# A two-layer encoder trunk on one core: one folded map at the start, value shifts issued by SyncE, the mask inside the running product, and dense matmuls pinned beside the last attention

## The chip, the core and the metric

The kernel runs on one core of a Trainium2 chip. A core has five engines with a queue each: TensorE (matmuls, PE in the profile; PEld is its weight load), VectorE (DVE), ScalarE (ACT), GpSimd (POOL) and SyncE (SP), which here does nothing but issue DMAs. ScalarE's queue can issue DMAs too. Each queue is worked off in order, so an instruction that waits holds back those behind it. Data lie in SBUF (128 partitions) and in DRAM; matmuls write to PSUM banks. The metric is the time of one execution in microseconds (us).

## The reference

All is float32: 2048 positions, 1024 channels, 16 heads of 64.

```
layer A: h = rms_norm(x); u, z = h @ w_in
         pooled = (trailing means of u over 2, 4, 8, 16 positions, by channel group) - u
         x += ((pooled per group @ w_group) * scale * silu(z)) @ w_out;  x += (p0 @ ple0) * sigmoid(x @ gate0)
k, v  = rms_norm(x) @ w_kv;  k = rms_norm per head
layer B: q, z = rms_norm(x) @ w_in;  q = rms_norm per head
         A[t,s] = beta[t,s] * prod_{s<j<t} (1 - beta[t,j]),  beta = sigmoid(q.k / 8),  only s < t
         o = A @ v;  x += (o * silu(z)) @ w_out;  x += (p1 @ ple1) * sigmoid(x @ gate1)
```

## The kernel before, in words

**Matmuls.** Each operand is split into a high part and the rest (`hi`, `lo`), and a product is three matmuls per 128 channels: hi x hi (L221), hi x lo (L223), lo x hi (L226). A dense product of 128 outputs by 512 positions is thus 24 matmuls of 512 columns in one PSUM bank `psd`. The first two products of a stage go through `product2` (L240, L242, L245); q, k and v through `kvq` (L467).

**Chunks.** The 2048 positions are four chunks of 512. For a chunk, `first_part` runs layer A: `mixer` (z and pooled u per group, 16 products), `out_steps` (8), `gate_steps` (8 and 8 small ones), then z of layer B (`gate_z`, 8) and q, k, v of heads 0 to 7; `second_part` runs q, k, v of heads 8 to 15. Before u is needed, `fold` multiplies the input map of a group with its group map (48 matmuls of 256 columns, L271), and the result `wf` goes to DRAM and comes back as weights.

**Attention** runs in slots (chunk c, head h, key chunk kc from c down to 0), each of four steps j, one per 128 queries. In a step `front` makes logits (L690, L691, bank `psl`), ScalarE their sigmoid of the negative (L693, `pp`), in the slot on the diagonal GpSimd sets the masked keys to 1 (L695), and VectorE runs the product along the keys from last to first (L697). `turn` transposes the result by four matmuls (L708, `psa`), ScalarE and VectorE split it into `at` (L711, L712), and `gather` multiplies with values (L720, L721, `pso`). Since A is a difference of two neighbours of the running product, the values enter as differences of neighbouring rows: `valued` (L480 to L490) makes a row-shifted copy `vs` of v by DMAs, on ScalarE's queue, stores the last row of each 128 (`ve`), and `load_ends` (L678) reads these back as `en`.

**What sets the order.** The code is one stream of dense matmuls (`stream`, a generator that yields after each) into which attention steps are cut: in each step `fill` draws a share of the stream that `rate` gives, 66 products per chunk spread over the chunk's steps. `until` runs the stream on to the mark after which a head's q, k, v exist. What is written so is then put in order by a scheduler, which may bring any instruction forward whose inputs it takes to be ready. After the last chunk's attention, `post(3)` (output projection and gate of layer B, 18 products' worth) is left. `post(0)` to `post(2)` are filler of the last attention.

**Weights** come as units, nine in flight (`UNITS`), in the order of a list `plan`: at first use raw from DRAM into an `io` buffer, cast and split by ScalarE with VectorE or GpSimd (L129 to L136), and stored once; later uses load the stored pair (L143). `io` also holds x, residuals and others.

Of the kernel before, what the change touches and what calls it, by code (L numbers as in the profile page):

```python
# [36 lines left out]
def trunk_kernel(ctx, tc, x, p, a_norm, wu_t, wz_a, w_group, a_scale, a_w_out, kv_norm, w_kv,  # L37
# [11 lines left out]
    zeros = cp.tile([P, 1], F32, name="zeros")  # L49
    V.memset(zeros, 0.0)  # L50
# [33 lines left out]
    io = flat("io", 5)  # L84
# [11 lines left out]
    state = {"solo": True, "turn": 0, "lo": 0}  # L96
# [27 lines left out]
    wq = {"out": 0, "back": 0, "cap": 2, "by": nc.scalar}  # L124
# [69 lines left out]
    for s in range(NSUB):  # L194
        if s == 0:
            plan_group(3)
            plan_group(2)
        for g in (3, 2, 1, 0):
            plan_block("za", wz_a, g, g_a, True)
            plan_block("wf", None, g)  # L200
            if s == 0 and g > 1:
                plan_group(g - 2)
# [47 lines left out]
    def fold(g):  # L250
        parts = {}
        raws = {}
        for h in range(2):
            for c in range(2):
                raws[c, h] = raw = io("uraw")
                nc.sync.dma_start(out=raw, in_=wu_t[2 * g + c, :, h * W5 : (h + 1) * W5])
        (wg, _), = take(1)
        for h in range(2):
            for c in range(2):
                raw = raws[c, h]  # L260
                hi, lo = ppt("uh", F32R), ppt("ul", F32R)
                A.copy(out=hi, in_=raw)
                V.tensor_tensor(out=lo, in0=raw, in1=f(hi), op=ALU.subtract)
                parts[c, h] = (hi, lo)
        for kts in PAIRS:
# [28 lines left out]
    def token_norm(total, nm):  # L294
        ps = turned()
        for j in range(4):
            T.matmul(ps[:, 0, j : j + 1], total[:, j * P : (j + 1) * P], ones, start=True, stop=True)
        ss = pool.tile([P, 4], F32, tag="ss" + nm, name="ss")
# [24 lines left out]
    def prep(s):  # L323
        ck = chunk[s]
        ck["x"] = []
        for o in range(KT):
# [8 lines left out]
            gather_squares(ck, "acc1", o, xin)  # L335
            yield
        r = token_norm(ck["acc1"], "x")
# [39 lines left out]
    def mixer(s):  # L377
        ck = chunk[s]
        ck["m"] = {}
        for g in (3, 2, 1, 0):  # L380
            us, zs = take(4), []
            for k in range(2):
                ps = dense()
                yield from product(ps, us, ck["x"], k * P, k)
                zs.append(silu(ps, ck["rb1"]))
            us = take(4)
# [4 lines left out]
            if s == 0 and g > 1:  # L391
                yield from fold(g - 2)
# [65 lines left out]
    def kvq(s, kind, b):  # L458
        ck = chunk[s]
        us = take(KT)  # L460
        for j in range(4):
            tk = slice(j * P, (j + 1) * P)
            ps = dense()
            for kt in range(KT):
                u = us[kt][0]
                for xh, wh in ((0, 0), (1, 0), (0, 1)):
# [4 lines left out]
                    yield  # L471
                if lag and (j, kt) in ((1, 2), (1, 5), (2, 1), (2, 4)):
# [5 lines left out]
    def valued(s, kind, b, j, ps, rj):  # L478
# [3 lines left out]
        for lo, hi in ((0, 112), (112, P - 1)):  # L482
            nc.scalar.dma_start(out=vs[lo + 1 : hi + 1], in_=vr[lo:hi])
        if j:
            nc.scalar.dma_start(out=vs[0:1], in_=chunk[s]["vr"][P - 1 : P])
        elif s:
            nc.scalar.dma_start(out=vs[0:1], in_=ve[s - 1][b][3:4])
        else:
            V.memset(vs[0:1], 0.0)
        nc.scalar.dma_start(out=ve[s][b][j : j + 1], in_=vr[P - 1 : P])  # L490
# [65 lines left out]
    def gate_z(s):  # L556
# [8 lines left out]
        us = take(4)  # L565
        pss = [dense(), dense()]
        yield from product2(pss, us, ck["x2"])
        first = []
        for k in range(2):
            zr = row("zr")  # L570
            A.copy(out=zr, in_=pss[k])
            first.append(zr)
        ck["r2"] = token_norm(ck["acc2"], "y")
        for b in range(1, 4):
            us = take(4)
            for k in range(2):
                o = 2 * b + k
                ps = dense()
                for i, _ in enumerate(product(ps, us, ck["x2"], k * P, k)):
                    if o == 2 and i == 20:  # L580
# [11 lines left out]
    def first_part(s):  # L592
# [6 lines left out]
        yield from every(gate_z(s), 48, ck["side"])  # L599
# [3 lines left out]
        marks.add((s, 0))  # L603

# [70 lines left out]
    def load_ends(c, b):  # L675
        en = pool.tile([P, 4, 4], F32, tag="en", name="en")
        for j in range(4):
            nc.scalar.dma_start(out=en[:, :, j], in_=ve[c][b][j].rearrange("(m q) -> q m", q=P))  # L678
# [5 lines left out]
    def front(st, j):  # L684
# [9 lines left out]
        if st["diag"]:  # L694
            G.affine_select(out=pp[:, W5 - P :], in_=pp[:, W5 - P :], pattern=[[-1, P]], compare_op=ALU.is_gt,  # L695
# [206 lines left out]
```

## Time and profile before

| | |
|---|---|
| median of 3 runs | 2842.41 us (2839.97 to 2845.93) |
| the profiled execution | 2844.09 us, its span 2842.3 us |
| granted TensorE clock, mean | 0.983 |
| busy: TensorE, VectorE, ScalarE, GpSimd | 2729.0, 1863.5, 1267.3, 1012.1 us |
| matmuls | 13344 |
| DMA | 651.86 MB, mean 229 GB/s |

A row of the grouped view has line, engine, operation, out<-in, shapes and count, then busy time in us and mean ns of one, then the engine's idle time before them and what ended most of it. A row of the timeline has start and duration in us, engine ("q" behind it: its sequencer, which issues DMAs), line, operation, names, count, and in brackets the idle time before it with its releaser. A row of the view by stretches has, for each engine, busy us and number of instructions. A row on a line's operation has the shortest, median and longest duration in ns, and the first and last start.

### The profile page before, as it was taken

The numbers are of one execution on the slowest core, as the hardware profiler recorded it, in microseconds if no ns is written. First come the engines' busy times: TensorE is split into PE (matmuls) and PEld (weight loads), VectorE is DVE, ScalarE is ACT, GpSimd is POOL, SyncE is SP. The second block draws the span as 40 slices with busy tenths as digits, with TensorE's granted clock in tenths as the row PEclk, the third lists the DMA queues.
The fourth block names the chain that finished last, engine by engine and source line by source line (L and its number), as shares of the span: only waits on it lengthen the run. The fifth ranks groups of instructions, "written<-read, shape, count | busy, mean of one in ns | idle before, by whom it ended". The sixth has DMA issues, their size and how long they took to land. (4 is left out here: it accounts for less than half of the span.)

```text
span 2842.3 us, 39230 instructions
## 1 busy us (share of the span) xinstructions
PE 2729.0 (96%) x13344; PEld 2247.5 (79%) x13344; DVE 1863.5 (66%) x2369; ACT 1267.3 (45%) x2498; POOL 1012.1 (36%) x961
## 2 busy tenths in 40 slices
PE   7999979989999999999999999999999999998889
PEld 6888867877878888887888877787788888886567
DVE  6745445757344787655577887665667777678962
ACT  5335443444444345444444554444444344445541
POOL 2454433767543355543324452323212121111112
PEclk9999999999999999999999999999999999999999
DMA  7748799878887745678684548457697776763335
GB/s 294 269 148 302 295 337 351 305 246 294 296 289 278 238 143 176 219 228 273 229 271 152 155 155 261 157 200 241 212 288 230 218 256 210 235 204 111 108 117 184
DMA packets 302804, 651.86 MB, mean 229 GB/s; under 512 B 51462, under 2 KB 84230, under 8 KB 302604
## 3 DMA queue, kind: packets, MB, share of 16 engines
q1 hardware_dynamic: 278080, 639.23, 67.9%
q10 hardware_dynamic: 24524, 10.11, 1.5%
q8 instruction: 106, 1.74, 0.3%
q14 instruction: 94, 0.77, 0.1%
HBM read 479.82 MB, written 161.02 MB: 225 GB/s over the span
## 5 line engine op out<-in xcount | busy, mean ns | idle before, releaser
L697 DVE TENSOR_TENSOR_SCAN pp<-pp,zeros 128x512 f32<-128x512 f32 (+3 forms) x640 | 778.5, 1236 | 239.1 <-ACT pp L693 118.9
L467 PE MATMUL psd<-wpair,x 128*128 128x512 f32 x2304 | 589.5, 398 | 17.5 <-ACT wpair L135 8.1
L467 PEld LDWEIGHTS psd<-wpair,x 128*128 128x128 f32 x2304 | 428.4, 190 | 108.8 <-ACT wpair L135 9.2
L712 DVE TENSOR_TENSOR at<-psa,at 128x512 fp32r<-128x512 f32 (+3 forms) x640 | 373.9, 597 | 198.4 <-ACT at L711 196.9
L711 ACT CAST at<-psa 128x512 fp32r<-128x512 f32 (+3 forms) x640 | 330.2, 525 | 376.0 <-PE psa L708 344.2
L693 ACT ACTIVATE pp<-psl 128x512 f32<-128x512 f32 (+3 forms) x640 | 325.3, 534 | 288.6 <-PE psl L691 149.5
L708 PE MATMUL psa<-ident,pp 128*128 128x128 f32 x2176 | 354.5, 279 | 47.7 <-DVE at L712 42.4
L708 PEld LDWEIGHTS psa<-ident,pp 128*128 128x128 f32 x2176 | 273.7, 143 | 135.4 <-DVE at L712 50.1
L695 POOL TENSOR_SCALAR_AFFINE_SELECT pp<-pp 128x128 f32<-128x128 f32 x256 | 119.1, 469 | 544.3 <-ACT pp L693 517.1
L721 PE MATMUL pso<-at,vv 128*128 128x512 f32 (+3 forms) x640 | 271.8, 425 | 0.2 <-DVE at L712 0.2
L690 PE MATMUL psl<-kk,qa 128*128 128x512 f32 (+3 forms) x640 | 244.4, 384 | 4.5 <-ACT pp L693 4.0
L720 PE MATMUL pso<-at,vv 128*128 128x512 f32 (+3 forms) x640 | 240.2, 376 | 6.5 <-ACT at L711 3.9
L691 PE MATMUL psl<-kk,qb 128*128 128x512 f32 (+3 forms) x640 | 234.7, 369 | 0.0
L221 PE MATMUL psd<-x,wpair 128*128 128x512 f32 x576 | 228.7, 397 | 4.9 <-ACT sg L443 3.4
L223 PE MATMUL psd<-x,wpair 128*128 128x512 f32 x576 | 227.3, 395 | 0.0
L226 PE MATMUL psd<-x,wpair 128*128 128x512 f32 x576 | 227.1, 394 | 0.0
L221 PE MATMUL psd<-xp,wpair 128*128 128x512 f32 x512 | 201.0, 393 | 1.4 <-DVE ub L356 0.6
L223 PE MATMUL psd<-xp,wpair 128*128 128x512 f32 x512 | 200.6, 392 | 0.0
L226 PE MATMUL psd<-xp,wpair 128*128 128x512 f32 x512 | 200.2, 391 | 0.0
L131 POOL TENSOR_TENSOR wpair<-wraw,wpair 128x512 fp32r<-128x512 f32 x98 | 142.3, 1458 | 93.3 <-ACT wpair L129 92.9
L690 PEld LDWEIGHTS psl<-kk,qa 128*128 128x128 f32 x640 | 122.4, 191 | 32.0 <-ACT pp L693 12.7
L720 PEld LDWEIGHTS pso<-at,vv 128*128 128x128 f32 x640 | 123.5, 193 | 24.6 <-ACT at L711 9.4
(159 smaller groups left out, 4761.4 us busy)
## 6 DMA issues: line engine op xcount, KB each, us to landing
wpair<-once SPq DMA_DIRECT2D x384, 512.0 KB, 5.6
once<-wpair SPq DMA_DIRECT2D x80, 512.0 KB, 6.5
kk<-kd SPq DMA_DIRECT2D x320, 128.0 KB, 3.4
vv<-vd SPq DMA_DIRECT2D x160, 256.0 KB, 4.0
wpair<-wf SPq DMA_DIRECT2D x64, 512.0 KB, 5.4
once<-kp SPq DMA_DIRECT2D x36, 512.0 KB, 5.4
wraw<-in_a_w_out_dram SPq DMA_DIRECT2D x64, 256.0 KB, 3.8
wraw<-in_gate_a_dram SPq DMA_DIRECT2D x64, 256.0 KB, 4.2
```

Source lines behind the costliest of these rows:

```text
L221: T.matmul(ps, hi, acts[kt][:, 0], start=(i == 0), stop=False)
L223: T.matmul(ps, hi, acts[kt][:, 1], start=False, stop=False)
L226: T.matmul(ps, lo, acts[kt][:, 0], start=False, stop=(i == n))
L467: T.matmul(ps, ck["x2"][kt][:, xh, tk], u[:, wh, 0], start=(kt == 0 and xh == wh), stop=(kt == KT - 1 and wh == 1))
L690: T.matmul(ps[:, :w], qa[:, qs], kk[:, :w], start=True, stop=False)
L693: A.activation(out=pp[:, r0:], in_=ps[:, :w], func=AF.Sigmoid, scale=-1.0)
L697: V.tensor_tensor_scan(out=pp[:, r0:][:, ::-1], data0=pp[:, r0:][:, ::-1], data1=zeros.to_broadcast([P, w]), initial=1.0 if st["diag"] els ...
L708: T.transpose(pt[:, j * P : (j + 1) * P], pp[:, r0 + kt * P : r0 + (kt + 1) * P], ident)
L711: A.copy(out=at[:, 0, cs], in_=pt[:, cs])
L712: V.tensor_tensor(out=at[:, 1, cs], in0=pt[:, cs], in1=f(at[:, 0, cs]), op=ALU.subtract)
L720: T.matmul(po[:, cs], vv[:, kt, :], at[:, 0, cs], start=(st["diag"] and kt == 0), stop=False)
L721: T.matmul(po[:, cs], vv[:, kt, :], at[:, 1, cs], start=False, stop=(st["last"] and kt == 3))
```

## The change

Six things are edited.

1. **Start.** The input map of group 3 alone is folded before x is read in; those of groups 2, 1 and 0 are loaded one group ahead (`fold_load`) and folded at the start of their own group, not two groups ahead. The sums of squares of the first chunk's x are made by 32 one-column matmuls (L355 in the new file) instead of additions on GpSimd. The first weights are asked for with a cap of 1, not 2.
2. **Shifts.** The DMAs of `valued` and `load_ends` are issued by SyncE instead of ScalarE.
3. **Mask.** The select on GpSimd (256 of them) goes. The running product takes the larger of the product and a floor, where it added zero: the floor is 0, and 1 at masked keys. It is a constant tile of 512 columns, and `io` has 4 buffers instead of 5.
4. **Last z.** In the last chunk `gate_z` runs after q, k, v of heads 0 to 7 and behind the mark that lets attention start. The norm it used to make is made in `kvq`.
5. **Rate.** Accordingly 58 products are spread over the third chunk's attention, and 74 over the last.
6. **Pins.** Beside the last attention, each first matmul of a weight unit in `product` stays behind the matmul written before it on TensorE.

```diff
-    zeros = cp.tile([P, 1], F32, name="zeros")
-    V.memset(zeros, 0.0)
+    floor = cp.tile([P, W5], F32, name="floor")
+    V.memset(floor, 0.0)
+    G.affine_select(out=floor[:, W5 - P :], in_=floor[:, W5 - P :], pattern=[[-1, P]], compare_op=ALU.is_gt,
+                    fill=1.0, base=0, channel_multiplier=1)
-    io = flat("io", 5)
+    io = flat("io", 4)
-    wq = {"out": 0, "back": 0, "cap": 2, "by": nc.scalar}
+    wq = {"out": 0, "back": 0, "cap": 1, "by": nc.scalar}
...
+        if s + 1 == NSUB:
+            plan_kvq(0)
         for b in range(4):
             plan_block("zb", b_w_z, b, g_b, True)
-        plan_kvq(0)
+        if s + 1 < NSUB:
+            plan_kvq(0)
...
-                T.matmul(ps, hi, acts[kt][:, 0], start=(i == 0), stop=False)
+                ins = T.matmul(ps, hi, acts[kt][:, 0], start=(i == 0), stop=False)
+                if state["pin"] and e == 0:
+                    tc.keep_in_program_order(ins)
...
+                sq = tmp("sq")
+                A.activation(out=sq, in_=xin, func=AF.Square)
+                if o == 0:
+                    sums = turned()
+                for j in range(4):
+                    tc.keep_in_program_order(
+                        T.matmul(sums[:, 0, j : j + 1], sq[:, j * P : (j + 1) * P], ones,
+                                 start=(o + j == 0), stop=(o == KT - 1 and j == 3)))
...
         for g in (3, 2, 1, 0):
+            if s == 0 and g < 3:
+                yield from fold(g)
...
+            if s == 0 and g:
+                fold_load(g - 1)
...
-            if s == 0 and g > 1:
-                yield from fold(g - 2)
...
+                if j == 0 and kt == 5 and "r2" not in ck:
+                    ck["r2"] = token_norm(ck["acc2"], "y")
...
-            nc.scalar.dma_start(out=vs[lo + 1 : hi + 1], in_=vr[lo:hi])
+            nc.sync.dma_start(out=vs[lo + 1 : hi + 1], in_=vr[lo:hi])
...
-        yield from every(gate_z(s), 48, ck["side"])
+        if s + 1 < NSUB:
+            yield from every(gate_z(s), 48, ck["side"])
         for kind in "qkv":
             yield from every(kvq(s, kind, 0), 48, ck["side"])
         settle()
         marks.add((s, 0))
+        if s + 1 == NSUB:
+            yield from gate_z(s)
...
-            nc.scalar.dma_start(out=en[:, :, j], in_=ve[c][b][j].rearrange("(m q) -> q m", q=P))
+            nc.sync.dma_start(out=en[:, :, j], in_=ve[c][b][j].rearrange("(m q) -> q m", q=P))
...
-        if st["diag"]:
-            G.affine_select(out=pp[:, W5 - P :], in_=pp[:, W5 - P :], pattern=[[-1, P]], compare_op=ALU.is_gt,
-                            fill=1.0, base=0, channel_multiplier=1)
-        V.tensor_tensor_scan(out=pp[:, r0:][:, ::-1], data0=pp[:, r0:][:, ::-1],
-                             data1=zeros.to_broadcast([P, w]),
-                             initial=1.0 if st["diag"] else st["carry"][j], op0=ALU.mult, op1=ALU.add)
+        least = floor[:, r0:][:, ::-1] if st["diag"] else floor[:, 0:1].to_broadcast([P, w])
+        V.tensor_tensor_scan(out=pp[:, r0:][:, ::-1], data0=pp[:, r0:][:, ::-1], data1=least,
+                             initial=1.0 if st["diag"] else st["carry"][j], op0=ALU.mult, op1=ALU.max)
...
-        return (66 * 24.0) / (64 * (c + 1) - (5 if c < NSUB - 1 else 0))
+        parts = 66 + (0, 0, -8, 8)[c]
+        return (parts * 24.0) / (64 * (c + 1) - (5 if c < NSUB - 1 else 0))
...
+            state["pin"] = slots[i][0] == NSUB - 1
```

**Where the order moves: the last attention.** On TensorE, at the transposes of the twelfth head of the last chunk; before:

```order
L708 MATMUL psa_25766<-ident_60,pp_25652 128x128
L708 MATMUL psa_25766<-ident_60,pp_25677 128x128
L708 MATMUL psa_25766<-ident_60,pp_25704 128x128
L721 MATMUL pso_25385<-at_25723,vv_25473 128x512
L690 MATMUL psl_25893<-kk_25726,qa_25499 128x512
L691 MATMUL psl_25893<-kk_25726,qb_25500 128x512
L690 MATMUL psl_25918<-kk_25726,qa_25499 128x512
L691 MATMUL psl_25918<-kk_25726,qb_25500 128x512
```

and now, at the same head:

```order
L736 MATMUL psa_24960<-ident_60,pp_24915 128x128
L749 MATMUL pso_24592<-at_24907,vv_24689 128x512
L721 MATMUL psl_24992<-kk_24827,qa_24714 128x512
L722 MATMUL psl_24992<-kk_24827,qb_24715 128x512
L230 MATMUL psd_24953<-og_24272,wpair_24590 128x512
L223 MATMUL psd_24953<-og_24274,wpair_24615 128x512
L227 MATMUL psd_24953<-og_24274,wpair_24615 128x512
L230 MATMUL psd_24953<-og_24274,wpair_24615 128x512
L223 MATMUL psd_24953<-og_24276,wpair_24615 128x512
L748 MATMUL pso_24592<-at_24932,vv_24689 128x512
```

The dense products (`psd`), which had run out four heads earlier, now stand between the steps. Counted from one head's first transposes to the next head's, the last chunk's first 15 heads have 132, 120, 120, 136, 128, 120, 136, 132, 122, 66, 6, 0, 6, 0, 6 dense matmuls before, and 90, 73, 101, 115, 102, 118, 109, 115, 106, 122, 101, 111, 111, 67, 6 now; behind the 16th stands what is left of the end. In the chunk before, where a head has 12 steps, the two leanest stretches of 16 steps go from 63 and 88 to 48 and 99.

**ScalarE's queue at the start** (`uh` is the high part of the input map, `wraw` and `wpair` the group map, `xp` the first x). Before:

```order
L146 DMA wraw_322<-in_a_w_group_dram 128x512
L262 ACT_TABLE_LOAD
L262 CAST uh_331<-uraw_313 128x512
L320 DMA xin_359<-in_x_dram 128x512
L262 CAST uh_335<-uraw_315 128x512
L320 DMA xin_363<-in_x_dram 128x512
L146 DMA wraw_327<-in_a_w_group_dram 128x512
L262 CAST uh_339<-uraw_317 128x512
L129 CAST wpair_321<-wraw_322 128x512
L776 DMA gains_103<-in_a_scale_dram 128x8
```

and now:

```order
L331 DMA xin_359<-in_x_dram 128x512
L266 CAST uh_332<-uraw_320 128x512
L148 DMA wraw_341<-in_a_w_group_dram 128x512
L806 DMA gains_106<-in_a_scale_dram 128x8
L266 CAST uh_336<-uraw_322 128x512
L806 DMA gains_106<-in_b_norm_dram 128x8
L806 DMA gains_106<-in_kv_norm_dram 128x8
L806 DMA gs_108<-in_k_norm_dram 128x1
L806 DMA gs_108<-in_b_q_norm_dram 128x1
L131 CAST wpair_340<-wraw_341 128x512
L119 CAST xp_496<-xin_345 128x512
```

One group map is loaded instead of two, behind the third cast, and its own cast stands behind the loads of the five gains. On TensorE, 24 of the 32 sums stand between the map's matmuls and the first dense one, the last eight 13 dense matmuls further.

**SyncE's queue at the first value block** (`vr` is a block of 128 value rows). Before, these DMAs were ScalarE's, and SyncE went from `qa`, `qb` to `once` and `wraw`. Now:

```order
L690 DMA qa_3637<-qd0_0_229 64x512
L515 DMA ve0_0_301<-vr_3396 1x512
L508 DMA vs_3398<-vr_3396 112x512
L508 DMA vs_3398<-vr_3396 15x512
L508 DMA vs_3464<-vr_3462 112x512
L508 DMA vs_3464<-vr_3462 15x512
L510 DMA vs_3464<-vr_3396 1x16x32
L515 DMA ve0_0_301<-vr_3462 1x512
L510 DMA vs_3519<-vr_3462 1x16x32
L148 DMA wraw_3559<-in_b_w_q_dram 128x512
```

The weight load `wraw` now waits in the queue behind the shifts of two value blocks. In all, 158 DMA issues (64 + 24 + 6 + 32 for the values, 32 for the row ends) leave ScalarE for SyncE.

More of the change, by code (lines that the diff above doesn't have):

```diff
@@ L563, in put @@
             nc.sync.dma_start(out=zd[s][o], in_=zr)
-        us = take(4)
-        pss = [dense(), dense()]
-        yield from product2(pss, us, ck["x2"])
         first = []
[L569 to L574, printed above, removed]
+        if "r2" in ck:
+            ck["rb2"] = bcast(ck["r2"], "y")
+        else:
+            us = take(4)
+            pss = [dense(), dense()]
+            yield from product2(pss, us, ck["x2"])
+            for k in range(2):
+                zr = row("zr")
+                A.copy(out=zr, in_=pss[k])
+                first.append(zr)
+            ck["r2"] = token_norm(ck["acc2"], "y")
+        for b in range(1 if first else 0, 4):
             us = take(4)
@@ L778, in trunk_kernel @@
                            op0=ALU.mult, op1=ALU.mult)
-    wq["by"] = nc.sync
-    for _ in start:
-        pass
-    side = prep(0)
-    for _ in range(4):
-        next(side)
-    wq["cap"] = UNITS
-    second = fold(2)
-    next(second)
-    for _ in range(4):
-        next(side)
-    for _ in second:
-        pass
-    for _ in side:
+    wq["cap"] = UNITS
+    for _ in fold(3):
+        pass
+    for _ in prep(0):
         pass
```

50 lines of the change are left out of this document (27 added, 23 removed).

## The prediction

> **What bounds the kernel now.** I read the stretches first: busy time of each engine between two points of the span, with the number of instructions behind each (columns PE, PEld, DVE, ACT, POOL, then granted clock, DMA share, GB/s).
>
> ```profile
> span 2842.3 us, 39230 instructions
> 0.00:40.00 40.00, 19.56 (x104) 18.88 (x105) 26.92 (x76) 23.20 (x47) 15.80 (x17) 0.83 0.62 216
> 100.00:200.00 100.00, 100.00 (x443) 82.79 (x442) 51.40 (x70) 35.80 (x62) 49.74 (x44) 1.00 0.53 171
> ...
> 340.00:430.00 90.00, 73.87 (x314) 56.83 (x313) 44.05 (x61) 38.33 (x70) 30.11 (x33) 0.91 0.99 332
> 560.00:700.00 140.00, 128.23 (x588) 105.36 (x587) 96.31 (x104) 69.32 (x141) 98.61 (x83) 0.96 0.81 261
> 1600.00:2060.00 460.00, 442.12 (x2210) 364.70 (x2209) 318.66 (x385) 221.01 (x435) 145.23 (x136) 0.98 0.63 201
> 2060.00:2552.00 492.00, 491.70 (x2498) 410.79 (x2497) 363.20 (x422) 210.28 (x411) 95.49 (x86) 1.00 0.74 236
> 2552.00:2740.00 188.00, 157.10 (x787) 116.59 (x785) 163.03 (x198) 104.88 (x212) 21.72 (x30) 0.93 0.38 111
> 2581.30:2643.30 62.00, 51.40 (x250) 37.80 (x250) 54.81 (x67) 35.12 (x71) 7.55 (x11) 0.89 0.37 107
> ```
>
> TensorE bounds most of it: in 100:200 it runs 443 matmuls back to back, 0.226 us each. The busy column flatters it, since ends are modelled, so I price TensorE by starts. A step of attention (one 128-query block of one slot) is four matmuls and four transposes; the chain of waits gives them, start to start.
>
> ```profile
> 2737.66 0.23 PE psl L690
> 2737.89 0.23 PE psl L691
> 2738.13 0.45 PE psa L708 x4
> ```
>
> So a full step is 4 x 0.23 + 0.45 = 1.37 us of TensorE. Pricing every matmul like this (0.226 for 512 columns, in proportion below, 0.11 for a transpose) gives about 2623 us of work in the span of 2842, so some 219 us are idle: 28 before 40 us, 27 in 340:430, 20 in 560:700, 38 in 1600:2060, 6 in 2060:2552, 58 in 2552:2740, the remaining 42 scattered. The question is how much of each the change takes.
>
> **The last attention**, where most of it lies. By 2552 the dense work that can be used as filler is spent, and VectorE decides:
>
> ```profile
> L697 DVE TENSOR_TENSOR_SCAN pp<-pp,zeros 128x512 f32<-128x512 f32 x78 | 97.6, 1278 | 7.7 <-ACT pp L693 7.0 <-POOL pp L695 0.5
> L712 DVE TENSOR_TENSOR at<-psa,at 128x512 fp32r<-128x512 f32 x78 | 51.9, 675 | 15.5 <-ACT at L711 15.5
> ```
>
> A step costs VectorE 1.28 + 0.68 = 1.96 us against TensorE's 1.37. The row 2581.30:2643.30 holds two heads of 16 steps: 62.0 us, 31.0 a head. TensorE's share of a head is 20.4 us (16 steps, four of them shortened by the diagonal), plus about 0.7 for three stray matmuls; 9.9 us of each such head is idle. With d dense matmuls beside a head, TensorE needs 20.4 + 0.226 d; it overtakes VectorE's 31 at about d = 47, somewhat later as dense work adds VectorE work too.
>
> The program order (counts in the section on the change) has five last-chunk heads with 0 or 6 dense matmuls before, and one now; all others but that one have 67 or more. So four heads lose 9.9 us each: **40 us**. The dense work is not created. It is the 192 matmuls of the last z, carried over from the chunk before, and the matmuls that used to run ahead of their place. What they leave is leaner: in the chunk before, the two leanest stretches of 16 steps go from 63 and 88 dense matmuls to 48 and 99, and the last chunk's first three have 90, 73 and 101 instead of 132, 120 and 120. Counted in pieces of eight steps, three pieces there now fall below VectorE's 1.9 us a step, by 4.2, 0.6 and 5.5 us, where none did; I charge 10.3, and 2 more for stalls of an order that no longer lets dense work slip ahead. Sum 40 - 12 = **28 us**. Lower bound 10: each of the nine heads between 73 and 111 loses 2 us as well. Upper bound 40: VectorE's queue averages the seam away.
>
> That the scan is dearer beside GpSimd matters for this margin:
>
> ```profile
> L697 DVE TENSOR_TENSOR_SCAN pp<-pp,zeros 128x512 f32<-128x512 f32 x106 | 153.2, 1479 | 56.9 <-ACT pp L693 44.4 <-POOL pp L695 12.2
> ```
>
> This is 2100:2500, where GpSimd is busier: 1479 ns instead of 1278. Even so 16 x (1.48 + 0.68) = 34.6 us a head stays under the 43 of TensorE at d = 100. The Trainium skill (SBUF — State Buffer, § Who interferes with whom) says that a VectorE instruction with two SBUF inputs and a GpSimd one that reads SBUF exclude each other, and the loser waits for the whole of the other. By it, each select dropped from a lean head could save a further 0.3 us, some 7 us over the six lean heads before; the 1278 ns in just those heads leaves next to nothing for it, and the sum leaves it out.
>
> **The start.** The reader is to see in the timeline that TensorE starts at 10.41, runs out of the first folded map at 18.9, and twice waits 5 us for pieces of the second.
>
> ```profile
> 8.52 0.34 ACTq L146 DMA_DIRECT2D wraw<-in_a_w_group_dram  x1
> 9.74 0.62 ACT L129 CAST wpair<-wraw 128x512 fp32r<-128x512 f32 x1 [0.22 <-DMA wraw<-in_a_w_group_dram]
> 10.41 0.58 PE L271 MATMUL psd<-wpair,uh 128*128 128x256 f32 x1 [10.41 <-ACT wpair L129]
> 14.46 0.36 ACTq L776 DMA_DIRECT2D gs<-in_b_q_norm_dram  x1
> 14.86 0.62 ACT L129 CAST wpair<-wraw 128x512 fp32r<-128x512 f32 x1 [3.99 <-DMA gains<-in_kv_norm_dram]
> 15.39 0.61 ACT L117 CAST xp<-xin 128x512 fp32r<-128x512 f32 x1
> 18.83 0.28 PE L271 MATMUL psd<-wpair,uh 128*128 128x256 f32 x1
> 23.97 0.50 PEld L271 LDWEIGHTS psd<-wpair,uh 128*128 128x128 f32 x2 [5.07 <-ACT uh L262]
> 29.94 0.29 PEld L271 LDWEIGHTS psd<-wpair,ul 128*128 128x128 f32 x1 [5.46 <-DVE ul L263]
> 31.39 1.70 PE L297 MATMUL pst<-ones,acc 128*128 128x1 f32 x8
> 16.03 3.67 DVE L118 TENSOR_TENSOR xp<-xin,xp 128x512 fp32r<-128x512 f32 x3 [3.76 <-ACT xp L117]
> ```
>
> Now the group weights are asked for once, at the place of the second load (8.5), and their cast stands behind the five gain loads, where the second cast stood at 14.86. So the first matmul comes **later**, at about 15, not 10.4. The map's 48 matmuls took 10.41 to 18.95, 8.5 us, most of them at the low clock: 23.5. Then 24 of the 32 new one-column sums; eight took 1.70 us at the low clock, and at full clock I put 0.11 on each: 2.7 us, 26.2. Are x and the z weights ready by then? ScalarE casts x from 15.4 at 0.52 us an operation, 14 of them: 22.7; the first two weight pieces 0.9 more: 23.6. VectorE's subtractions were 1.22 us each beside GpSimd's squares (3.67 for three), which are gone. So dense work runs from 26.2 without the two holes. Until 40 us that makes 48 x 0.12 + 13.8 - 0.9 (the last eight sums) = 18.6 us of useful work, where before 92 fold matmuls and four dense ones (of the row's 104) made 12: a gain of **6.6**. Bounds: 0, if each of the three later maps, now folded one group ahead instead of two, makes TensorE wait about 2 us for its trip through DRAM; 11, if the first matmul stays at 10.4.
>
> **The mask and the shifts** act in the first chunk.
>
> ```profile
> 377.40 4.21 PE L467 MATMUL psd<-wpair,x 128*128 128x512 f32 x9 [7.49 <-ACT wpair L135]
> 375.14 0.39 ACTq L678 DMA_DIRECT2D en<-ve  x1
> 375.62 0.62 ACT L498 CAST vv<-vs 128x512 fp32r<-128x512 f32 x1 [7.91 <-DMA once<-wpair]
> 419.64 0.42 DVE L697 TENSOR_TENSOR_SCAN pp<-pp,zeros 128x128 f32<-128x128 f32 x1 [3.70 <-POOL pp L695]
> L483 ACTq DMA_DIRECT2D vs<-vr x64: 518/838/1375, 338.7 to 2056.6; - x64
> L695 POOL TENSOR_SCALAR_AFFINE_SELECT pp<-pp 128x128 f32<-128x128 f32 x256 | 119.1, 469 | 544.3 <-ACT pp L693 517.1
> ```
>
> At 367.7 (375.62 less 7.91) ScalarE's queue stops at a load of row ends whose source is still on its way to DRAM; the weight casts behind it wait, and TensorE stands for 7.49 us. That load is now SyncE's. At 419.64 a scan waits 3.70 us for a select; all 256 selects go. Together 11 us of the 27 idle in 340:430. But DMA share there is 0.99, so part of what is not lost to the queue will be lost to weights landing late: I take **7**. SyncE pays: it gets 158 issues more, and the first value block holds it while it waits for two products (24 x 0.226 = 5.4 us each) with weight loads behind. Lower bound -11, two such holds in full; upper +15, with half of what 560:700 loses. Elsewhere the wait is covered by nine weight units of 12 matmuls, 24 us. Beyond the first chunk ScalarE loses 64 x 0.84 = 54 us of issue, nearly all off the path: **2**. The scan itself I keep at its price: same elements, max for add; a second input read in full instead of a broadcast is unseen in this trace, and at 256 diagonal scans even 0.1 us more lies under TensorE. One buffer fewer for raw weights is in the lower bound.
>
> The Trainium skill (DMA: Bandwidth & Descriptors, § Issuing engines are not separate DMA queues) speaks against expecting more from the move: transfers of either queue share the same 16 DMA engines, so only issue time is saved. By it this term is the 11 us of queue holds at most; the 0.99 agrees.
>
> **Sum:** 28 + 6.6 + 7 + 2 = 43.6. The profiled execution took 2844.1, 1.7 above the median of the three times (2842.4), so **2801** for the changed kernel.
>
> **Rivals.** *The seam eats it.* More lean heads where the last two chunks meet, each losing 3 to 5 us on VectorE: the last attention nets 10, the start 4, the first chunk 3: 2827. For it: the 38 us idle of 1600:2060 already lie there; against it: most heads keep above 100.
> *The order does not hold on the chip:* dense work that is not pinned (the wide q, k, v products) still runs ahead and the last heads stay bare; only start and first chunk gain: 2829. The order, with one bare head, speaks against it.
> *SyncE becomes the brake, slower than before.* Every one of the eight value blocks makes SyncE wait on four products, weights and keys queue behind, and the cover of 24 us does not hold, since waits for earlier transfers sit in the same queue. It decides from the point at which a block costs TensorE more than 4.6 us ((28 + 6.6 + 2) / 8); at 6 each: 2844 - 37 + 48 = 2855. For it: 0.99 DMA share in the first such block; against it: in the three later chunks the share is 0.63 to 0.81.
>
> **Chances.** Forecast 0.68 (own range 2778 to 2820), seam 0.13, order 0.06, SyncE 0.09; 0.04 beyond. The range 2776 to 2832 takes in seam and order and leaves out SyncE. Faster by over 0.2% (5.7 us, about what this kernel's times can tell apart): 0.86; within: 0.05; slower: 0.09.
>
> **What would show it.** Right: one bare head at the end, scans 1.28 us there; 2552:2740's idle 58 us down to under 20; first matmul near 15, no hole of 5 us before 40; no 7 us hole at 377. Wrong: holes on TensorE ended by weight loads while SyncE waits on value rows; idle in the first heads of the last chunk above 20 us; folds waiting for wf loads in 40:150.

## The result

The changed kernel takes **2828.24 us** (median of four runs, 2823.22 to 2831.42) against 2844.17 for the kernel before (four runs): a ratio of 0.9942, 95% interval 0.9923 to 0.9961. It is faster, and by 16 us, not by the 43.6 forecast.

To see where, I compare the two traces at equal work: every matmul is priced by start-to-start time as in the prediction, and the table gives how much later (+) or earlier (-) a kernel has done so many us of that work than the kernel before. The one-column sums are priced at nothing, since the changed kernel has 56 records more of them, which are no progress. The two profiled executions lie 12.7 us apart (2831.4 and 2844.1), so the table ends there and not at 16.

```
work done, us           10    40   120   300   600  1320  1860  2400  2520   end
changed kernel        +2.6  +3.9 +20.8 +20.8 +16.0 +17.2 +20.4 +28.8 -12.5 -12.7
```

The last attention (2400 to 2520) gives 41.3 us, about as forecast, and the first chunk's attention (300 to 600) 4.8, where 7 were forecast. Between 1320 and 2400, where the last two chunks meet, 12 are lost. But the start, which was to give 6.6, costs 20.8: 3.9 by 40 us of work, 16.9 more between 40 and 120. The stretches of the changed kernel (columns as in the prediction) show the same; the last row is the kernel before.

```profile
0.00:40.00 40.00, 25.69 (x130) 24.05 (x131) 16.63 (x70) 19.08 (x39) 3.49 (x10) 0.81 0.72 250
40.00:160.00 120.00, 110.84 (x518) 92.27 (x517) 65.81 (x120) 44.07 (x87) 34.02 (x34) 0.92 0.71 244
340.00:430.00 90.00, 79.17 (x356) 63.00 (x355) 46.22 (x64) 40.78 (x70) 30.68 (x29) 0.96 0.94 324
560.00:700.00 140.00, 128.19 (x583) 104.89 (x582) 91.81 (x105) 69.54 (x143) 85.93 (x61) 0.95 0.77 246
1600.00:2060.00 460.00, 439.48 (x2229) 363.38 (x2227) 333.06 (x404) 228.77 (x458) 124.95 (x90) 0.99 0.60 193
2060.00:2552.00 492.00, 483.61 (x2481) 400.29 (x2482) 366.21 (x442) 229.42 (x445) 71.59 (x50) 1.00 0.69 223
2552.00:2740.00 188.00, 180.98 (x921) 146.09 (x920) 148.89 (x175) 89.78 (x175) 17.82 (x11) 0.98 0.59 186
```

```profile
40.00:160.00 120.00, 120.00 (x580) 101.39 (x580) 79.12 (x133) 47.52 (x92) 46.65 (x46) 1.00 0.77 279
```

In 40:160 TensorE did 580 matmuls before and 518 now. The timeline of the changed kernel's start shows the first matmul, the new sums, and three stops, each at the first matmul on a folded map (in brackets the idle time and what ended it; the second stop is put down to VectorE, but the semaphore it waits for is that of a `wpair<-wf` load issued at 108.57):

```profile
7.38 0.34 ACTq L148 DMA_DIRECT2D wraw<-in_a_w_group_dram  x1
13.64 0.62 ACT L131 CAST wpair<-wraw 128x512 fp32r<-128x512 f32 x1 [4.70 <-DMA gains<-in_kv_norm_dram]
14.31 0.58 PE L279 MATMUL psd<-wpair,uh 128*128 128x256 f32 x1 [14.31 <-ACT wpair L131]
...
21.65 7.60 PE L355 MATMUL pst<-ones,sq 128*128 128x1 f32 x48
29.11 0.77 PE L223 MATMUL psd<-xp,wpair 128*128 128x512 f32 x1
...
40.77 0.63 PE L227 MATMUL psd<-xp,wpair 128*128 128x512 f32 x1
41.20 0.58 PE L230 MATMUL psd<-xp,wpair 128*128 128x512 f32 x1
41.62 0.39 PE L223 MATMUL psd<-xp,wpair 128*128 128x512 f32 x1
...
80.30 0.77 PE L223 MATMUL psd<-xp,wpair 128*128 128x512 f32 x1 [3.30 <-DMA wpair<-wf]
80.86 0.63 PE L227 MATMUL psd<-xp,wpair 128*128 128x512 f32 x1
81.29 0.63 PE L230 MATMUL psd<-xp,wpair 128*128 128x512 f32 x1
...
114.03 0.77 PE L223 MATMUL psd<-xp,wpair 128*128 128x512 f32 x1 [3.22 <-DVE wpair L138]
...
147.02 0.47 PE L223 MATMUL psd<-xp,wpair 128*128 128x512 f32 x1 [2.30 <-DMA wpair<-wf]
```

The three stops cost 9.3 us start to start, and the matmuls behind each run 0.43 us apart (80.86 to 81.29) instead of 0.23, 7 to 13 of them: 6.4 us more. That is 15.7 of the 16.9 us lost between 40 and 120 us of work.

What is lost before that stands in the rows from 21.65 to 41.62. The 24 sums ahead of the dense work are 48 records, two for each, and hold TensorE for 7.5 us (21.65 to 29.11). The dense matmuls behind them then run 0.43 us apart until 41.20. In the first 40 us of the span the changed kernel does 9.5 us of useful work, the kernel before 11.3.

### The profile page after: what moved, and what is told of

Read it like the earlier page. It is cut to its first block, busy times and chain, and to the rows that moved or that the text cites. A ratio compares the mean times of both kernels' runs of the same rounds, so it can differ in the third digit from the quotient of the medians.

```text
span 2829.6 us, 38580 instructions
## 1 busy us (share of the span) xinstructions
PE 2731.6 (97%) x13400; PEld 2257.3 (80%) x13400; DVE 1846.1 (65%) x2369; ACT 1272.0 (45%) x2496; POOL 878.4 (31%) x699
## 4 chain that ended last, share of the span: by engine, by line
PE 68%; DVE 4%; DMA 4%; issue 1%; ACT 1%; POOL 1%; SPq 0%; ACTq 0%; DVEq 0%; POOLq 0%
PE psd L490 14%; PE psd L223 9%; PE psd L227 9%; PE psd L230 9%; PE psa L736 7%; PE pso L749 4%; PE pso L748 4%; PE psl L722 4%; PE psl L721 4%; DVE pp L726 2%; PE psd L244 2%; PE psd L249 2%; PE psd L246 2%; DMA wpair<-once 1%; DMA kk<-kd 1%
## 5 line engine op out<-in xcount | busy, mean ns | idle before, releaser
L726 DVE TENSOR_TENSOR_SCAN pp<-pp,floor 128x512 f32<-128x512 f32 (+3 forms) x640 | 769.7, 1220 | 166.5 <-ACT pp L724 164.5
L721 PE MATMUL psl<-kk,qa 128*128 128x512 f32 (+3 forms) x640 | 243.8, 382 | 11.3 <-DMA kk<-kd 6.5
L223 PE MATMUL psd<-x,wpair 128*128 128x512 f32 x592 | 233.4, 394 | 2.5 <-ACT sg L466 2.5
L227 PE MATMUL psd<-x,wpair 128*128 128x512 f32 x592 | 232.6, 393 | 0.0
L230 PE MATMUL psd<-x,wpair 128*128 128x512 f32 x592 | 232.1, 392 | 0.0
L223 PE MATMUL psd<-xp,wpair 128*128 128x512 f32 x512 | 206.2, 403 | 8.8 <-DMA wpair<-wf 5.6
L227 PE MATMUL psd<-xp,wpair 128*128 128x512 f32 x512 | 205.3, 401 | 0.0
L230 PE MATMUL psd<-xp,wpair 128*128 128x512 f32 x512 | 204.3, 400 | 0.0
L459 POOL TENSOR_TENSOR xj<-x 128x512 f32<-128x512 f32 x64 | 105.4, 1650 | 141.9 <-DVE sg L470 137.7
L764 POOL TENSOR_TENSOR os<-os,zt 128x512 f32<-128x512 f32 x32 | 46.3, 1446 | 306.3 <-ACT os L763 247.6
```

Source lines behind the costliest of these rows:

```text
L223: ins = T.matmul(ps, hi, acts[kt][:, 0], start=(i == 0), stop=False)
L227: T.matmul(ps, hi, acts[kt][:, 1], start=False, stop=False)
L230: T.matmul(ps, lo, acts[kt][:, 0], start=False, stop=(i == n))
L721: T.matmul(ps[:, :w], qa[:, qs], kk[:, :w], start=True, stop=False)
L726: V.tensor_tensor_scan(out=pp[:, r0:][:, ::-1], data0=pp[:, r0:][:, ::-1], data1=least, initial=1.0 if st["diag"] else st["carry"][j], op0 ...
```

## Experiments: what costs the start

Four theories. **T1:** one group's lead is too short for a folded map's way out to DRAM and back. **T2:** the buffer for raw weights (`io`) that went makes weights late. **T3:** SyncE's queue, now with the shifts, holds them. **T4:** the loss lies in the last attention. The times at equal work below are those of the table's method, against the kernel before.

Part 1 of the change undone in the changed kernel:

```diff
-            if s == 0 and g < 3:
-                yield from fold(g)          # head of its own group
+            if s == 0 and g > 1:
+                yield from fold(g - 2)      # two groups ahead; old start, squares on GpSimd
```

> The changed kernel with the first part alone undone: maps 3 and 2 folded beside x, maps 1 and 0 two groups ahead, squares summed by GpSimd, as in the kernel before. T1 (the start lost what it was to gain: with only one group's lead, each later folded map's way out to DRAM and back holds TensorE): the 17 us lost by 150 us come back, 2805 to 2813 us. T2 (the io pool of four buffers, which this kernel keeps, makes the raw weights late in the first chunk): no more than 4 us back, 2824 to 2828. T3 (the SyncE queue, now with the shifts, holds the weights): 2824 to 2828 too. T4 (what was lost lies in the last attention, not at the start): 2828 plus the start's 6 us, 2834.

Measured 2811.7 (0.9900, 0.9871 to 0.9928): the 17 us come back, and T4 falls. Next, part 1 alone in the kernel before, with its five buffers:

> The kernel before with the first part alone: map 3 alone ahead of x, maps 2, 1 and 0 each folded at the head of its own group, squares summed by TensorE; five io buffers, shifts by ScalarE, mask by GpSimd as before. T1: slower than before by about 17 us, 2858 to 2865, with TensorE stopped at three places between 60 and 150 us on the folded maps. T2 (four io buffers): here there are five, so the prediction's own +6.6 holds, 2834 to 2840. T3 (SyncE's queue with the shifts): the same, 2834 to 2840.

Measured 2840.0 (0.9994, 0.9979 to 1.0010). This refutes T1 as it stood, with its 17 us: at 40 us of work this kernel is 4.9 us ahead, at 120 level (0.0), with stops of 0.6 and 1.0 us on a folded map. With five buffers the new fold place eats what the beginning won, and no more; with four the start loses. So the map's way should matter much only while the buffers make it late, and an earlier fold should cure it:

```diff
-            if s == 0 and g < 3:
-                yield from fold(g)
+            if s == 0 and g:
+                fold_load(g - 1)
             us, zs = take(4), []
...
             if s == 0 and g:
-                fold_load(g - 1)
+                yield from fold(g - 1)      # between z and u of the group ahead
```

> The changed kernel with each of maps 2, 1 and 0 folded half a group earlier, between the z products and the u products of the group ahead of its own, its weights loaded one half group earlier too; map 3 alone ahead of x as in the changed kernel. T1: the way through DRAM then has one group's half more (11 us) to lie in, the three stops of 3 to 6 us at 80, 114 and 147 us go, and the start's gain of 6 us stays: 2803 to 2814 us. T2 and T3 (late raw weights or a full SyncE queue): the stops stay, or come back as waits on raw weights, 2824 to 2832.

Measured 2813.1 (0.9899, 0.9873 to 0.9926), no stop on a map left: 3.6 us behind at 40 us of work, and still 3.7 at 120. And the buffer given back in the changed kernel (the row of scales `rb` gives up one of its two):

```diff
-    io = flat("io", 4)
+    io = flat("io", 5)
```

> The changed kernel with five buffers for raw weights again instead of four (the 2 KB come from the broadcast row of scales, which has one buffer instead of two). The runs so far leave two causes for the 17 us lost by 150 us: the fold's new place by itself is cleared, since it gains 3 to 8 us beside five buffers. T2 (four buffers and the new fold place together: loads of z weights wait for raw map tiles, and the folded maps' stores stand behind them in SyncE's queue): the first matmul is back at 10.4 us, the three stops at 80, 114 and 147 shrink to 1 us or none, 2805 to 2812. T3 (the new mask, shifts or last z do it in another way): 2824 to 2832.

Measured 2814.9 (0.9887, 0.9860 to 0.9913); at 120 us of work it is 21.0 ahead of the changed kernel, that is 0.2 ahead of the kernel before (5.0 at 40). The other way round, part 1 in the kernel before and `io` at 4:

> The kernel before with the first part of the change and four buffers for raw weights instead of five; mask, shifts and the last attention as before. T2 (the two together cost what was lost): first matmul at 14.3 us, stops at 80, 114 and 147, 20 us slower than the same kernel with five buffers: 2854 to 2864. T3: 2834 to 2842, as with five.

Measured **2868.7** (1.0081, 1.0060 to 1.0103), with stops of 3.7, 3.6 and 1.9 us at 77, 110 and 142: 14.1 behind at 120 us of work. T2 holds together with the new fold place, and T3 falls: here there are no shifts on SyncE. Either cure, the buffer or the earlier fold, takes away the long stops. The timeline of five buffers, at the start and on SyncE's queue:

```profile
3.58 0.34 ACTq L148 DMA_DIRECT2D wraw<-in_a_w_group_dram  x1
9.49 0.61 ACT L131 CAST wpair<-wraw 128x512 fp32r<-128x512 f32 x1
10.16 0.58 PE L279 MATMUL psd<-wpair,uh 128*128 128x256 f32 x1 [10.16 <-ACT wpair L131]
...
42.67 0.42 SPq L262 DMA_DIRECT2D uraw<-in_wu_t_dram  x1
48.70 0.50 SPq L262 DMA_DIRECT2D uraw<-in_wu_t_dram  x1
59.50 1.33 SPq L289 DMA_DIRECT2D wf<-wf  x2
62.18 1.64 SPq L145 DMA_DIRECT2D wpair<-wf  x2
69.67 1.26 SPq L145 DMA_DIRECT2D wpair<-wf  x2
```

The same queue in the changed kernel:

```profile
39.49 4.03 SPq L145 DMA_DIRECT2D wpair<-wf  x2
51.35 0.32 SPq L152 DMA_DIRECT2D once<-wpair  x1
51.72 0.43 SPq L148 DMA_DIRECT2D wraw<-in_wz_a_dram  x1
53.07 0.41 SPq L262 DMA_DIRECT2D uraw<-in_wu_t_dram  x1
58.82 0.38 SPq L262 DMA_DIRECT2D uraw<-in_wu_t_dram  x1
72.08 1.63 SPq L289 DMA_DIRECT2D wf<-wf  x3
74.77 1.66 SPq L145 DMA_DIRECT2D wpair<-wf  x2
```

With five buffers the group weights are asked for at 3.58, beside the four map tiles that fill the other buffers; with four only at 7.38. Later one z weight (51.72) is still to be loaded when the next map's tiles are due. In SyncE's queue it and they stand behind the store at 51.35, which waits 7.8 us for VectorE's split of another z weight: 53.07 instead of 42.67. Ten us late, the folded map is stored 12.6 us late and loaded back 12.6 late. The late beginning is 8.9 of these (5.0 ahead against 3.9 behind at 40 us of work); the 3.7 left are about the stop of 3.5 at 80.3.

What the buffer costs by itself, in the kernel before with `io` at 4 and nothing else:

> The kernel before with four buffers for raw weights instead of five and nothing else changed. If one buffer costs only together with the new place of the folds: within 3 us of before up to 300 us of the span, and 2840 to 2846 in all. If it also makes weights late in the first chunk's attention: 5 to 10 us lost between 340 and 700, 2846 to 2854.

Measured **2858.6** (1.0057, 1.0041 to 1.0072). At the old start it costs nothing (-0.5 us at 300), in the first chunk's attention 12 us (+11.6 at 660). Its stretches:

```profile
340.00:430.00 90.00, 74.63 (x323) 55.98 (x322) 44.04 (x63) 41.25 (x74) 33.77 (x37) 0.96 0.97 336
560.00:700.00 140.00, 123.39 (x555) 100.53 (x554) 91.99 (x104) 66.78 (x138) 91.49 (x82) 0.95 0.76 244
```

In 560:700 it does 555 matmuls where the kernel before did 588.

## Experiments: mask and shifts

Both alone in the kernel before, with four buffers:

```diff
-            nc.scalar.dma_start(out=vs[lo + 1 : hi + 1], in_=vr[lo:hi])
+            nc.sync.dma_start(out=vs[lo + 1 : hi + 1], in_=vr[lo:hi])
-            G.affine_select(out=pp[:, W5 - P :], ...)
+        least = floor[:, r0:][:, ::-1] if st["diag"] else floor[:, 0:1].to_broadcast([P, w])
```

> The kernel before with the mask in the running product and the shifts and row ends by SyncE alone; four buffers for raw weights, the old start. Prediction's terms: 7 us in the first chunk and 2 elsewhere: 2831 to 2836. If the four buffers cost by themselves wherever they are: no gain before 300 us and some loss there, 2840 or more. If SyncE becomes the brake: 2845 or more, with stops of TensorE near 377 and 560.

Measured 2822.0 (0.9924, 0.9907 to 0.9942): 21 us, 5 of them by 600 us of work and 12 between 1620 and 1860, where I had 2 for everything outside the first chunk. One at a time, the mask with four buffers, the shifts with five, the mask with five:

> The kernel before with the mask in the running product alone (four buffers for raw weights, GpSimd's select gone). Mask and shifts together gave 21 us: 5 in the first chunk and some 13 between 1600 and 1860 us, where the prediction had 2. If the selects' waits on the path are what counts: 8 to 14 us here, 2828 to 2834, with half the gain after 1600. If the mask only frees GpSimd, which is off the path: within 4 us, 2838 to 2846. The program order of this kernel also has 130 dense matmuls in the stretch that had 63, so a gain between 1700 and 1800 us of 5 to 10 us belongs to the order, not to the select.

> The kernel before with the shifts and row ends issued by SyncE alone (five buffers, select by GpSimd as before). If the queue holds of ScalarE are what counts: the 7 us stop near 377 is gone, 5 to 8 us in the first chunk, and some 5 to 10 later, where the stretch with 63 dense matmuls has 106: 2828 to 2836. If SyncE pays with late weights: within 3 us of before, 2839 to 2846. With the mask's gain these should add up to the 21 us of both together.

> The kernel before with the mask in the running product alone, as in the run of the mask alone, but with five buffers for raw weights (the row of scales has one instead of two). There the mask lost 7 us by 660 us and won it back after 1600. If the fourth buffer's loss is what ate it in the first chunk: 6 to 10 us better than with four, 2830 to 2834. If the mask itself is worth nothing in the first chunk: 2837 to 2843.

Measured 2839.4 (0.9991, 0.9980 to 1.0002), 2825.5 (0.9951, 0.9934 to 0.9968) and 2824.7 (0.9936, 0.9916 to 0.9955). So the mask is worth 18 us, of which the buffer that its tile took eats 15; the shifts are worth 17. With four buffers the totals nearly add up (3 and 17 against 21), but not by place: between 1620 and 1860 the four kernels win 9 to 14 us each, both parts together no more than one, and in each the stretch with 63 dense matmuls has 106 or more in the program order. So I take that gain to come from the order, which the scheduler makes anew for every kernel; no run has the one without the other.

SyncE did not become the brake. From the changed kernel's waits of SyncE in 330:600 (us in total, times, longest):

```profile
SPq L508 <- ACT vr L505: 0.8, 1, 0.8
```

Over the whole kernel such waits of a shift for its value rows come to 12.6 us in seven times, the longest 4.7, and the shifts alone on SyncE gained 17.

## Experiments: the last attention and the seam

The parts on the last attention alone (last z, rates, pins) in the kernel before:

> The kernel before with the parts on the last attention alone: last z behind q, k and v, the new rates, and the dense matmuls pinned beside the last attention. If the account by equal work is right, the seam costs 10 to 12 us and the last attention gives 40 to 42: 2812 to 2818 us. If the mask in the running product and the shifts by SyncE are what made the last attention shorter, rather than the dense work that now reaches its last heads: 2835 or more.

Measured 2825.6 (0.9945, 0.9929 to 0.9961): the end gives 40, but between 1620 and 2400 us of work twenty are lost, not twelve. The pins taken out of the changed kernel:

```diff
-                if state["pin"] and e == 0:
-                    tc.keep_in_program_order(ins)
```

> The changed kernel without the pins on dense matmuls beside the last attention; rates and the last z as changed. The program order then has three last-chunk heads with 0 or 6 dense matmuls and one with 42, where the changed kernel has one with 6 and one with 67. If bare heads cost 9.9 us each as predicted: 20 us lost at the end, some 6 won back at the seam, whose first heads have 90, 177 and 120 dense matmuls again: 2838 to 2846. If the chip takes the same time in either order, because the same work is done anyway: 2826 to 2830.

Measured 2839.6 (0.9992, 0.9982 to 1.0002): bare heads are back, 21 us of idle at the end. The pins carry half of the last attention's gain; the kernel is 11 us slower than the changed one, not 21, and 6 of the rest are won back by 2400 us of work. With five buffers and the last chunk's rate at 68 parts, so that no head is bare, and the same with the earlier folds:

```diff
-        parts = 66 + (0, 0, -8, 8)[c]
+        parts = 66 + (0, 0, -8, 2)[c]
```

> The changed kernel with five buffers and the last chunk's rate at 68 parts instead of 74; folds where the changed kernel has them. If a bare head costs 9.9 us: 8 to 12 us better than five buffers alone (2814.9), so 2803 to 2808. If the thinner stretches (74 to 111 instead of 101 to 122) lose as much as the bare head gave: 2812 to 2818.

> The changed kernel with five buffers, each later map folded half a group earlier, and the last chunk's rate at 68 parts instead of 74, so that no last-chunk head has fewer than 74 dense matmuls in the program order (the changed kernel has one with 6 and one with 67). T2 for the start (five buffers suffice): like e12, within 4 us. T1 in its remainder (the trip still costs what is left of the stop at 107, 1.6 us, and low clock): 2 to 6 us better than e12. Time: 2796 to 2806.

Measured 2816.7 (0.9909, 0.9894 to 0.9924) and 2810.8 (0.9891, 0.9875 to 0.9907). The rate by itself brought nothing that can be measured (2816.7 against 2814.9), and the seam stayed. The next three, all with five buffers, ask what makes the seam: rates that leave no lean piece ahead of the last chunk (on top of the earlier folds), the old rates, the old place of the last z.

```diff
+        parts = 66 + (0, 0, 3, -10)[c]      # spread rates
+        parts = 66                          # old rates
-            yield from gate_z(s)            # old last z: ahead of q, k, v again
```

> As the best so far (five buffers, maps folded half a group earlier), with the rates 69 and 56 parts in the last two chunks' attention instead of 58 and 68 (74 in the changed kernel). In the program order no piece of eight steps in the chunk before the last has fewer than 33 dense matmuls (the changed kernel has one with 0 and two with 39), and the last chunk's heads have 51 to 99. If lean pieces in that order make the seam: TensorE's idle time in the nine stretches of 16 steps around it, 49 us with five buffers, falls under 35 and the time is 2796 to 2804. If the seam comes from the last z behind q, k and v (whose products keep their new place here): idle stays at 45 or more, 2808 to 2816.

> The changed kernel with five buffers and the rates of before (66 parts in every chunk); last z and pins as changed. If the rates make the seam: its idle time falls from 49 us to about 35, and the end loses one bare head and thinner heads, some 15 us: 2812 to 2822. If the last z makes it: seam unchanged, 2822 to 2832.

> The changed kernel with five buffers and the last z back ahead of q, k and v; rates and pins as changed. If the last z behind q, k and v makes the seam: its idle time falls from 49 us to 35 or less, 2798 to 2808. If the rates make it: seam as it was (the program order even has a stretch with 23 dense matmuls and its first last-chunk heads with 77 and 73), 2814 to 2824.

Measured **2801.7** (0.9861, 0.9843 to 0.9879), 2810.1 (0.9885, 0.9868 to 0.9903) and 2803.0 (0.9868, 0.9851 to 0.9884). Last, spread rates with the old last z:

> As the kernel with spread rates (five buffers, maps folded half a group earlier, rates 69 and 56), with the last z back ahead of q, k and v. If the last z's new place costs 10 us whatever the rates: TensorE's idle time at the seam 16 to 20 us, 2789 to 2795. If it cost only because it left a lean stretch, which the spread rates fill: seam 24 to 30 us as before, 2797 to 2804, no difference from the kernel with spread rates.

Measured 2801.7 (0.9863, 0.9844 to 0.9881), the same. TensorE's idle time (us, time less priced work) by stretches of 16 steps, steps 288 to 431 being the seam, 544 on the end (both kernels with spread rates also have the earlier folds):

```
steps                         288-431   432-543   544 on
before                          34.2       4.0     61.6
mask and shifts alone           26.0       4.8     59.9
attention parts alone           50.2       6.3     22.4
changed                         45.8       4.8     21.1
changed, no pins                44.5       4.1     42.6
five buffers                    49.4       9.4     22.7
  and old rates                 36.1       7.5     33.5
  and old last z                39.0       5.4     21.1
  and spread rates              26.5      19.9     26.8
  and spread rates, old last z  28.4      21.1     24.2
```

Rates make 13 us of the seam and the last z 10, and with spread rates the z's place makes no difference: it is the lean stretches. Their price is not what I charged. One with 39 dense matmuls (of the kernel with five buffers) took 39 us with 10.4 idle, while VectorE was busy 74% of it: it has the next chunk's elementwise work beside the steps. That this comes in lumps is how I explain the idle time; no run tests it. The stretch 1700:1860 of that kernel, then of spread rates:

```profile
1700.00:1860.00 160.00, 150.29 (x745) 123.51 (x744) 115.19 (x143) 77.81 (x156) 38.99 (x31) 0.95 0.61 199
```

```profile
1700.00:1860.00 160.00, 159.48 (x818) 132.58 (x817) 107.97 (x132) 76.84 (x150) 40.49 (x33) 1.00 0.76 253
```

## Why the prediction was right or wrong

**The start failed: +6.6 forecast, -20.8 measured.** That is 27 of the 31 us by which the forecast of 43.6 missed the 12.7 between the two traces. Two steps are at fault.

The first is that the sum puts the trip of the three later maps through DRAM at nothing. It appears in the lower bound alone, at "about 2 us" each, where a stop took 3.1 on average and the slow matmuls behind it 2.1: 15.7 for the three. What made it so dear is the sentence "One buffer fewer for raw weights is in the lower bound": I had put that bound (-11) on mask and shifts, and left the buffer out of the start, where it decides whether maps arrive. With five buffers the same fold place costs 4.8 between 40 and 120 us of work, with the earlier fold and five buffers nothing (4.4 ahead at 40, 4.3 at 120). The last of the signs that I had listed against myself, folds waiting for wf loads in 40:150, is what came.

The second is the time until dense work runs. "24 of the 32 new one-column sums" at 0.11 each gave 2.7 us and 26.2; the trace has 48 records for them and 7.5 us, so that dense work began at 29.11 although the map was done at 21.65, earlier than the 23.5 forecast. The eight records at L297, from which I took the price, were four sums. Then I counted 13.8 us at full clock, and TensorE ran at half until 41.20. Useful work in the first 40 us of the span: 18.6 forecast, 9.5 measured. With five buffers it is 16.7, a gain of 5.4 over the kernel before, though the first matmul comes at 10.16, where my bound of 11 stood for that case. The largest lead at 120 us of work in any run is 4.8 (spread rates): the 6.6 was never reached.

The Trainium skill (TensorE: Matmul & The Clock Gate, § What's actually happening) says that an idle window of some 3.4 us halves the clock until a busy one has passed; that agrees with the 0.43 us spacing here, for 5.7 us after the first stop, but a stop of 2.5 us was enough for it too.

**The first matmul** came at 14.31, forecast 15, for the reason given: its cast (13.64) stands behind the last of the five gain loads (issued at 13.26). What I had not seen is that having four buffers, not five, puts it there. With five the weights are asked for at 3.58, the cast runs at 9.49, and the last three gain loads are issued behind it.

**The last attention** held: 40 forecast for four heads no longer bare, 40.5 measured (61.6 less 21.1 idle), one bare head left; 2552:2740 is idle for 17 us by the prediction's pricing, 58 before, forecast under 20. In the bare head (the changed kernel's groups in 2671:2699) 13 full scans took 1350 ns, where I had said 1.28 us:

```profile
L726 DVE TENSOR_TENSOR_SCAN pp<-pp,floor 128x512 f32<-128x512 f32 x13 | 17.1, 1350 | 2.0 <-ACT pp L724 2.0
```

Over all 640 scans the mean fell from 1236 to 1220 ns, so the tile of floors did no harm.

**The seam** looked right (12 charged, 11.6 measured against the kernel before), by two errors that cancel: mask and shifts take 8 us out of it, and the lean stretches cost 20 against that. My rule for a lean piece, steps at VectorE's 1.9 us, leaves out VectorE's other work beside the steps.

**Mask and shifts in the first chunk**: 7 forecast, 4.6 measured by 660 us of work; 340:430 has 356 matmuls where 314 ran, and of 7.8 us won by 590 us of work 3 are lost again in the gate stage. **Elsewhere**: 2 forecast; 15 in the run of both alone (3.8 ahead at 660, 18.6 at 2520), hidden by the seam in the changed kernel.

**The rivals.** The seam's 2827 came closest to the measured time, but its account does not hold: its start gained 4, and its last attention netted 10 where 29 were measured. The order held on the chip, and SyncE did not brake. That five buffers, earlier folds and spread rates land on 2801.7, my 2801, is partly chance: that kernel is 37 us ahead at 1860, 3 at 2400 after its thinner last attention, and 45 at its end. Of the forecasts for the eighteen runs, nine missed the nearest of their ranges, by 2 to 9 us.

## What to carry to other kernels

A buffer taken from a pool is a change of its own: price it at every place that draws on the pool, above all where several loads are bunched, and in an in-order queue ask what stands behind the load or store that will wait. Take the price of a small operation from a row whose count you have checked against the code. Price a stop of TensorE with the slow matmuls behind it, here two thirds more. Filler work should be spread so that no stretch runs dry, counted against all the work of the next slowest engine, not against its steps alone.

## What was not expected of the hardware

Half speed came after stops shorter than 3 us: after 2.46 us at 147.02, seven matmuls lost 1.4 us; the stop of 1.9 us at 142 in the run of part 1 with four buffers was not followed by it. It came without a stop too: in the changed kernel one-column sums followed the map's matmuls without a gap at 21.65, TensorE was busy all the time by its rows, and the matmuls behind the sums ran 0.43 us apart. The same shows with five buffers (sums from 18.23 to 24.84, then 0.43 until 28.40); a run that separates the sums from the start was not made. And one buffer of 2 KB per partition more or less, in a kernel that has 39000 instructions, moved the time by 16 us (2858.6 against 2842.7) without a single operation changed. Why the first chunk's attention loses 12 of these with ScalarE's queue holding the shifts, and none between the changed kernel and its five buffers (4.6 and 3.0 won from 300 to 660 us of work), was not tried.
